# Up projection of a hybrid transformer block: four of seven partial products with joined matmuls

## The chip, the cores and the metric
The kernel runs on one core of one Trainium2 chip. The metric is device time in microseconds (us) of one execution. TensorE (PE) does the matmuls and loads its weights in a separate step (PEld), VectorE (DVE) and ScalarE (ACT) do elementwise work, GpSimd (POOL) and SyncE (SP) issue most of the DMAs. Each engine works through its own list of instructions in order and waits on semaphores for the others.

## The reference
One layer over 512 latent tokens and 256 context tokens of width 2048: modulated RMSNorm, an input projection that feeds an attention branch and a short convolution, an output projection with gated residual, then the gated MLP that this change is about, then a final norm.

```
def conv_ffn(h, w_up, cw, cb, w_down):
    u = dwconv3(h @ w_up, cw, cb)          # h: 512 x 2048, w_up: 2048 x 11008
    a, g = jnp.split(u, 2, axis=-1)
    return (a * jax.nn.silu(g)) @ w_down   # 5504 x 2048
```

Everything is float32. A product is formed from float32r halves: each operand is split into a high part and a low remainder, and the product is hi·hi + hi·lo + lo·hi.

## The kernel before, in words
**The up projection.** Its 11008 columns are 86 tiles of 128, taken in pairs f (one tile of the gate g, one of a). The pairs 0 to 2 are done in rows, k by k, with all 512 tokens per matmul (`row`, tiles `uf`). The pairs 3 to 42, 40 blocks in all, are done by a Strassen scheme of seven products over two halves of the tokens, two halves of the input width and the two column tiles. A block's products are p1 ("11"), p2 ("21"), p6 ("2"), q5 ("1"), p7 ("3"), and, one block later, q4 ("4") and q3 ("22") in `finish`. TensorE's order is p1, p2 of block f, q4, q3 of block f-1, p6, q5, p7 of block f.

Each product (`product`) splits 128x1024 weights into a high part on ACT (L998) and a low part on DVE (L999), and runs eight steps of `mm3` (L185 to L189): three matmuls of 256 columns, that is hi·x_hi, hi·x_lo, lo·x_hi, all into columns 0 to 255 of one PSUM bank. `u19p6l` is the low part of product p6 of block 19. Three buffers of high and of low weights are in turn. The x operands are `hf` (the normed input) and `T` (sums of its halves, made in `t_sums`), each with a tile for the high and one for the low part over 512 tokens.

**What DVE and ACT do with a product.** ACT copies p1, p6 and p7 aside (L1174); DVE makes `cg` from p2 (L1212) and q3 (L1182), and `ca` from q5 (L1224); ACT makes the rest of `ca` from q4 (L1180). `acts` runs the convolution (L1005 to L1007), silu and the gating product (L1015) on `cg` and `ca`. DVE also forms the weight sums of the next products (L1213, L1214).

**What is sent out.** Two finished blocks make a pair, whose seven sums (`pair_sums`, `put`, L1040 to L1044) go to DRAM (`t_d`) as operands of the down projection: ACT casts the high part (L1042), DVE forms the low part (L1043), POOL issues the write. They stand in a queue `bg`, of which `pump(1)` after every product takes one step. The tiles `tp` come from the pool t2, in which two buffers are left for them once `hf` and `T` are all made; a cast into one waits for the write from two puts before.

**The order.** Within what the code asks for, a scheduler sets each engine's list when the program is built. `issue_after` makes one instruction stand behind another in it.

**After the up projection** the down projection does seven tiles plainly (tiles `d`, 512 columns), then 24 steps of the same scheme (tiles `v`), and the final norm.

Of the kernel before, what the change touches and what calls it, by code (L numbers as in the profile page):

```python
# [10 lines left out]
F32 = mybir.dt.float32  # L11
F32R = mybir.dt.float32r
AF = mybir.ActivationFunctionType
ALU = mybir.AluOpType
# [3 lines left out]
P = 128  # L18
D = 2048
T = 512  # L20
# [11 lines left out]
G = 6  # L32
# [40 lines left out]
def block_kernel(ctx, tc, xt, ctxt, ctxn, c, c_ctx, w_ada, small, w_in, w_inc, w_q, w_kv, w_out,  # L73
# [23 lines left out]
    def t2(shape, dt, name):  # L97
        return act.tile(shape, dt, tag="t2", bufs=NT2, name=name)
# [37 lines left out]
        return ap.to_broadcast([P, n])  # L136

    spare = {}
    nth = {"raw": 0, "w": 0}

    ordered = [True]

# [36 lines left out]
    def part(w, i, n=1):  # L179
        return tuple(z[:, i * P:(i + n) * P] for z in w)  # L180
# [4 lines left out]
    def mm3(ps, w, x, first, last, on_top=False):  # L185
        with tc.issue_after(behind.pop()) if behind else ExitStack():
            PE.matmul(ps, w[0], x[0], start=first, stop=False, skip_group_check=on_top)  # L187
        PE.matmul(ps, w[0], x[1], start=False, stop=False, skip_group_check=on_top)  # L188
        PE.matmul(ps, w[1], x[0], start=False, stop=last, skip_group_check=on_top)  # L189


    bg, post, late_bg = deque(), [], []

    def pump(n=1):
        while n and bg:
            if next(bg[0], bg) is bg:
                bg.popleft()
            else:
                n -= 1
# [430 lines left out]
    with ExitStack() as pb:  # L630
# [238 lines left out]
        def bank_of(i, nm):  # L869
            return p8.tile([P, 512], F32, tag=f"s{i}", bufs=1, name=nm)  # L870
# [41 lines left out]
    def whole(raw, xs, nm, ps=None, cols=slice(0, T), ld=None, often=False):  # L912
# [10 lines left out]
            pump(1)  # L923
        return ps

    hf = {}


    hf_last = [None, None]

    def hf_tile(j, cols=slice(0, T)):
        if j not in hf:
# [7 lines left out]
        hi, lo = (z[:, cols] for z in hf[j])  # L940
        A.copy(out=hi, in_=xr)
        ins = V.tensor_tensor(out=lo, in0=xr, in1=hi.bitcast(F32), op=ALU.subtract)
        hf_last[:] = hf_last[1], ins.ins

    def hf_early():
# [89 lines left out]
    def pair_sums(p, e, o):  # L1035


        t = tmp([P, T], F32, f"ts{p}") if p == PAIRS - 1 else cp.tile([P, T], F32, tag="ts", bufs=1, name=f"ts{p}")

        def put(n, src):  # L1040
            z = t2([P, T], F32R, f"tp{p}{n}")
            A.copy(out=z[:, :256], in_=src)  # L1042
            V.tensor_tensor(out=z[:, 256:], in0=src, in1=z[:, :256].bitcast(F32), op=ALU.subtract)  # L1043
            G_.dma_start(t_d[p, OPS.index(n)], z.bitcast(F32))  # L1044

        put("11", e[:, H0])
# [28 lines left out]
    def t_sums(j):  # L1075

        e, o = xres[2 * j], xres[2 * j + 1]
        i, c = j // 2, HS[j % 2]
        if j % 2 == 0:
            for n in (1, 2, 4):  # L1080
                TT[n, i] = tuple(t2([P, T], F32R, f"T{n}{i}{z}") for z in "hl")

        def put(dst, src):
            hi, lo = dst
            A.copy(out=hi, in_=src)
            V.tensor_tensor(out=lo, in0=src, in1=hi.bitcast(F32), op=ALU.subtract)

        V.tensor_tensor(out=e[:, H0], in0=e[:, H0], in1=e[:, H1], op=ALU.subtract)
        V.tensor_tensor(out=e[:, H1], in0=o[:, H1], in1=e[:, H1], op=ALU.subtract)
        put(half_of(hf[2 * j], 1), e[:, H1])  # L1090
        V.scalar_tensor_tensor(out=o[:, H1], in0=e[:, H0], scalar=-1.0, in1=o[:, H1], op0=ALU.mult, op1=ALU.subtract)
        V.scalar_tensor_tensor(out=o[:, H0], in0=o[:, H1], scalar=-1.0, in1=o[:, H0], op0=ALU.mult, op1=ALU.subtract)
        for n, src in ((1, e[:, H0]), (2, o[:, H1]), (4, o[:, H0])):
            put(tuple(z[:, c] for z in TT[n, i]), src)

    def operand(n, j):
        if n in ("11", "3"):
            return half_of(hf[2 * j], n == "3")
        if n in ("21", "22"):
            return half_of(hf[2 * j + 1], n == "22")  # L1100
        return half_of(TT[int(n), j // 2], j % 2)

    def first_weights(k, held=False):

# [8 lines left out]
    def up_load(f):  # L1113
# [7 lines left out]
                G_.dma_start(r[-1], src[more], accum_op=ALU.add)  # L1121
        return r

    pss = [bank_of(i, f"uf{g}") for g, i in enumerate((2, 3, 4, 5, 1, 0))]
    held = [first_weights(k, k > 2) for k in range(EARLY)]
    for k in range(3, EARLY):
        hf_tile(k, H0)
    for k in range(EARLY):
        row(pss, held[k], hf[k], k, H0)
        pump(1)  # L1130
    drain()
    for k in range(EARLY):
        hf_tile(k, H1)
        row(pss, held[k], hf[k], k, H1)
        pump(1)
        if k in (3, 5):
            t_sums(k // 2 - 1)
# [9 lines left out]
    for k in range(EARLY, NK):  # L1147
        w = nxt
        if k + 1 < NK:
            if k == NK - 4:  # L1150
                raws = up_load(G // 2)
            if k == NK - 2:
                t_sums(sums.popleft())
            nxt = prepare(k + 1)
        row(pss, w, hf[k], k)
        if k % 2:
            sums.append(k // 2)
            t_sums(sums.popleft())
# [3 lines left out]
    bank8 = in_turn(BANKS)  # L1162
    one_bank[0] = bank8

    def product(ps, a, n, nm, first):

        w = split4(a, 1024, nm)
        for j in range(8):
            mm3(ps[:, :256], part(w, j), operand(n, j), first and j == 0, j == 7, on_top=not first)
        pump(1)  # L1170

    def aside(ps, nm):
        r = cp.tile([P, 256], F32, tag="uu", bufs=4, name=nm)
        A.copy(out=r, in_=ps[:, :256])  # L1174
        return r

    def finish(st):
        f, a22, s4, u2, u3, pa, pc, cg, ca = st
        product(pa, a22, "4", f"u{f}q4", False)
        A.activation(ca[:, H0], pa[:, :256], AF.Identity, scale=-1.0)  # L1180
        product(pc, s4, "22", f"u{f}q3", False)
        V.tensor_tensor(out=cg[:, H1], in0=pc[:, :256], in1=u2, op=ALU.add)  # L1182
        acts(f, cg, ca)


# [13 lines left out]
    for f in range(G // 2, NF):  # L1199
        a11, a12, s1, s3, a22 = raws  # L1200
        if f + 1 < NF:
            raws = up_load(f + 1)
        else:
            for _ in range(AHEAD):
                plain_fetch()
        pa, pb, pc = (bank8(f"u{f}{z}") for z in "abc")
        cg = cp.tile([P, T], F32, tag="cg", bufs=2, name=f"cg{f}")
        ca = cp.tile([P, T], F32, tag="ca", bufs=2, name=f"ca{f}")
        product(pa, a11, "11", f"u{f}p1", True)
        u1 = aside(pa, f"u{f}1")  # L1210
        product(pb, a12, "21", f"u{f}p2", True)
        V.tensor_tensor(out=cg[:, H0], in0=pb[:, :256], in1=u1, op=ALU.add)  # L1212
        V.tensor_tensor(out=a11, in0=a11, in1=s1, op=ALU.add)  # L1213
        V.tensor_tensor(out=a12, in0=a12, in1=a11, op=ALU.add)  # L1214
        if pend is not None:
            finish(pend)
        if first_acts and f == G // 2:
            acts(*first_acts.pop(0))
        product(pa, a11, "2", f"u{f}p6", False)
        u2 = aside(pa, f"u{f}2")  # L1220
        product(pc, s1, "1", f"u{f}q5", True)
        product(pa, s3, "3", f"u{f}p7", False)
        u3 = aside(pa, f"u{f}3")
        V.scalar_tensor_tensor(out=ca[:, H1], in0=pc[:, :256], scalar=-1.0, in1=u3, op0=ALU.mult, op1=ALU.subtract)  # L1224
        if first_acts:
            acts(*first_acts.pop(0))
        pend = f, a22, a12, u2, u3, pa, pc, cg, ca
# [366 lines left out]
```

## Time and profile before
| | us |
|---|---|
| median of 3 runs | 2151.49 |
| lowest, highest | 2147.65, 2155.0 |
| the profiled execution, its own time | 2158.83 |
| span of its instructions | 2157.0 |
| TensorE busy in the span | 2104.9 |
| VectorE busy | 1769.0 |
| ScalarE busy | 1047.1 |

The granted TensorE clock is 0.994 of full speed over the span. A row of the timeline has an instruction's start and its length; matmuls overlap, so that what one takes of TensorE's time is the distance from its start to the next one's. VectorE's and ScalarE's records overlap a little too.

### The profile page before, as it was taken

Reading aid. Unit: us, or ns where it says so; the run is one execution under the profiler, and the core shown is the slowest. Engines: PE = TensorE matmul, PEld = TensorE weight load, DVE = VectorE, ACT = ScalarE, POOL = GpSimd, SP = SyncE. Lnnn points to the kernel's source line nnn. Section 1 sums busy time; section 2 is a strip of 40 time slices with the busy share of each in tenths; the row PEclk is TensorE's granted clock in tenths of the full one; section 3 lists DMA queues with packets and bytes.
Section 4 is the critical chain, followed back from the end, with each engine's and each line's share of the span. In section 5 each row is a group of like instructions: output and inputs, shape, how many; then the busy total and the mean of one; then the engine's idle time right before and its main releaser. Section 6 shows DMA issues by size and latency. Waiting matters only on the chain.

```text
span 2157.0 us, 37744 instructions
## 1 busy us (share of the span) xinstructions
PE 2104.9 (98%) x14458; PEld 1946.7 (90%) x14458; DVE 1769.0 (82%) x2859; ACT 1047.1 (49%) x1710; POOL 188.1 (9%) x270
## 2 busy tenths in 40 slices
PE   7899999999999999999999999999999999999997
PEld 4688788888888888999999999999999889999997
DVE  7998987778886889788888788788888658888877
ACT  5533333555552237555555555555555333333445
POOL 0000000000000000111211111111111000000000
PEclk9999999999999999999999999999999999999998
DMA  9979785334559986577887877877887999877683
GB/s 335 345 275 337 270 279 176 128 126 162 177 199 348 344 278 192 159 217 201 241 232 215 240 229 220 237 231 219 241 229 218 341 335 290 254 220 236 196 247 111
DMA packets 162121, 513.89 MB, mean 238 GB/s; under 512 B 18962, under 2 KB 23314, under 8 KB 156306
## 3 DMA queue, kind: packets, MB, share of 16 engines
q1 hardware_dynamic: 133364, 418.14, 56.5%
q0 software_dynamic: 27488, 92.29, 18.3%
q8 instruction: 113, 1.85, 0.3%
q10 hardware_dynamic: 1088, 1.05, 0.1%
q14 instruction: 68, 0.56, 0.1%
HBM read 464.22 MB, written 46.14 MB: 237 GB/s over the span
## 4 chain that ended last, share of the span: by engine, by line
PE 86%; DVE 6%; DMA 5%; issue 1%; ACT 1%; SPq 0%; DVEq 0%; POOLq 0%; ACTq 0%
PE pp L187 4%; PE pp L189 4%; PE pp L188 4%; PE o L189 1%; PE o L187 1%; PE o L188 1%; DMA ada<-in_w_ada 1%; PE d L187 1%; PE d L189 1%; PE d L188 1%; PE uf L187 1%; PE uf L188 1%; PE of L187 1%; PE of L188 1%; PE of L189 1%
## 5 line engine op out<-in xcount | busy, mean ns | idle before, releaser
L1044 POOL DMA_DIRECT2D t_d<-tp x126 | 71.9, 574 | 468.3 <-DVE tp L1043 465.4
L255 DVE SCALAR_TENSOR_TENSOR ada<-ada,sv 128x1024 f32<-128x1024 f32 x68 | 82.1, 1219 | 12.1 <-DMA ada<-in_w_ada 12.0
L166 ACT CAST w_0h<-rw 128x512 fp32r<-128x512 f32 (+1 forms) x63 | 38.3, 618 | 108.3 <-PE pp L188 63.1
L1121 POOL DMA_DIRECT2D u_s<-in_w_up x80 | 70.2, 878 | 224.4 <-DMA u_s<-in_w_up 131.5
L233 DVE SCALAR_TENSOR_TENSOR ada<-ada,sv 128x1024 f32<-128x1024 f32 x64 | 77.5, 1217 | 4.4 <-DMA ada<-in_w_ada 3.9
L522 DVE SCALAR_TENSOR_TENSOR ada<-ada,svc 128x1024 f32<-128x1024 f32 x64 | 76.0, 1220 | 2.3 <-DMA ada<-in_w_ada 2.3
L785 POOL TENSOR_TENSOR gr<-gr,half 128x8 f32<-128x8 f32 x4 | 10.1, 2524 | 628.7 <-DVE gr L784 536.8
L1042 ACT CAST tp<-a 128x256 fp32r<-128x256 f32 x90 | 34.7, 405 | 60.5 <-DMA t_d<-tp 54.1
L167 DVE TENSOR_TENSOR w_0l<-rw,w_0h 128x512 fp32r<-128x512 f32 (+1 forms) x63 | 42.6, 681 | 22.3 <-ACT w_0h L166 22.3
L255 DVE SCALAR_TENSOR_TENSOR ra<-ra,sv 128x1024 f32<-128x1024 f32 x44 | 52.5, 1217 | 1.1 <-DMA ra<-in_w_ada 1.1
L1213 DVE TENSOR_TENSOR u<-u,u_s 128x1024 f32<-128x1024 f32 x40 | 48.8, 1219 | 0.7 <-DMA u_s<-in_w_up 0.7
L1214 DVE TENSOR_TENSOR u<-u,u 128x1024 f32<-128x1024 f32 x40 | 48.7, 1218 | 0.0
L1043 DVE TENSOR_TENSOR tp<-a,tp 128x256 fp32r<-128x256 f32 x90 | 36.2, 418 | 12.3 <-ACT tp L1042 12.3
L756 ACT CAST pth<-t 128x384 fp32r<-128x384 f32 x64 | 28.6, 485 | 26.4 <-PE t L753 26.4
L1042 ACT CAST tp<-ts 128x256 fp32r<-128x256 f32 x36 | 14.6, 407 | 43.5 <-DMA t_d<-tp 41.1
L533 DVE TENSOR_TENSOR acc<-acc,pp 128x512 f32<-128x512 f32 x50 | 34.0, 680 | 2.1 <-PE pp L189 2.1
L757 DVE TENSOR_TENSOR ptl<-t,pth 128x384 fp32r<-128x384 f32 x64 | 33.2, 549 | 2.7 <-ACT pth L756 2.7
L737 DVE TENSOR_REDUCE mn<-s 128x1 f32<-128x768 f32 x32 | 30.4, 952 | 4.8 <-PE s L726 4.6
L1043 DVE TENSOR_TENSOR tp<-ts,tp 128x256 fp32r<-128x256 f32 x36 | 15.2, 421 | 23.3 <-ACT tp L1042 23.3
L1005 ACT ACTIVATE g<-cg,sm 128x512 f32<-128x512 f32 x40 | 32.5, 813 | 0.5 <-DVE cg L1182 0.5
L1005 ACT ACTIVATE a<-ca,sm 128x512 f32<-128x512 f32 x40 | 32.1, 803 | 0.0
L1013 ACT ACTIVATE g<-g 128x512 f32<-128x512 f32 x43 | 27.2, 632 | 6.4 <-DVE g L1007 6.4
(15967 smaller groups left out, 9398.2 us busy)
## 6 DMA issues: line engine op xcount, KB each, us to landing
ada<-in_w_ada SPq DMA_DIRECT2D x196, 512.0 KB, 6.0
u<-in_w_up SPq DMA_DIRECT2D x120, 512.0 KB, 8.2
w<-t_d SPq DMA_DIRECT2D x161, 256.0 KB, 5.2
u_s<-in_w_up SPq DMA_DIRECT2D x80, 512.0 KB, 4.3
u_s<-in_w_up POOLq DMA_DIRECT2D x80, 512.0 KB, 8.9
t_d<-tp POOLq DMA_DIRECT2D x126, 256.0 KB, 4.9
v<-in_w_dnw SPq DMA_DIRECT2D x72, 384.0 KB, 5.4
ra<-in_w_ada SPq DMA_DIRECT2D x22, 1024.0 KB, 4.9
```

Of the source, the lines that this page charges most:

```text
L187: PE.matmul(ps, w[0], x[0], start=first, stop=False, skip_group_check=on_top)
L188: PE.matmul(ps, w[0], x[1], start=False, stop=False, skip_group_check=on_top)
L189: PE.matmul(ps, w[1], x[0], start=False, stop=last, skip_group_check=on_top)
L233: V.scalar_tensor_tensor(out=r, in0=r, scalar=1.0, in1=vec[:, i * 1024:(i + 1) * 1024], op0=ALU.mult, op1=ALU.mult, accum_out=col[:, i:i + 1])
L255: keep(V.scalar_tensor_tensor(out=r, in0=r, scalar=1.0, in1=svs[i], op0=ALU.mult, op1=ALU.mult, accum_out=lc[:, t % 4:t % 4 + 1] if i else ...
L522: keep(V.scalar_tensor_tensor(out=raw[q], in0=raw[q], scalar=1.0, in1=svc[:, q * 1024:(q + 1) * 1024], op0=ALU.mult, op1=ALU.mult, accum_o ...
L1005: A.activation(u, src, AF.Identity, bias=s("fb", m), scale=s("fw", 86 + m))
L1042: A.copy(out=z[:, :256], in_=src)
L1043: V.tensor_tensor(out=z[:, 256:], in0=src, in1=z[:, :256].bitcast(F32), op=ALU.subtract)
L1044: G_.dma_start(t_d[p, OPS.index(n)], z.bitcast(F32))
L1121: G_.dma_start(r[-1], src[more], accum_op=ALU.add)
L1213: V.tensor_tensor(out=a11, in0=a11, in1=s1, op=ALU.add)
```

## The change
In the products "21", "1", "4" and "22" the first two matmuls of each step, which have the same weights, become one of 512 columns (`mm2`, L196), for which x_hi and x_lo stand side by side in one tile; the third keeps 256 (L197). The bank then holds hi·x_hi + lo·x_hi in columns 0 to 255 and hi·x_lo in columns 256 to 511, and a new DVE instruction (`beside`, L1207) adds or subtracts the second half after the first has been used. The operands "21" and "22" (odd `hf` tiles) and "1", "2", "4" (`T`) are laid out so; "11" and "3" (even tiles) stay apart. For odd k the row-wise part works by 256 columns.

Beside this, `pump` takes a step after every second product, each third `tp` comes from a buffer of its own (`tq`), its cast stands behind the last high cast of weights, and `ca` has one buffer in place of two.

```
+    def mm2(ps, w, x, first, last, on_top=False):
+        n = x.shape[1] // 2
+        with tc.issue_after(behind.pop()) if behind else ExitStack():
+            PE.matmul(ps[:, :2 * n], w[0], x, start=first, stop=False, skip_group_check=on_top)
+        PE.matmul(ps[:, :n], w[1], x[:, :n], start=False, stop=last, skip_group_check=on_top)
...
+    def side_by_side(z, src):
+        n = T // 2
+        A.copy(out=z[:, :n], in_=src)
+        return V.tensor_tensor(out=z[:, n:], in0=src, in1=z[:, :n].bitcast(F32), op=ALU.subtract)
...
         def put(n, src):
-            z = t2([P, T], F32R, f"tp{p}{n}")
-            A.copy(out=z[:, :256], in_=src)
+            nth["tp"] += 1
+            if nth["tp"] % 3 or p == PAIRS - 1:
+                z = t2([P, T], F32R, f"tp{p}{n}")
+            else:
+                z = cp.tile([P, T], F32, tag="tq", bufs=1, name=f"tp{p}{n}")
+            with tc.issue_after(last_hi[0]):
+                A.copy(out=z[:, :256], in_=src)
...
+    def up_row(w, k, hs=(0, 1)):
+        if k % 2 == 0:
+            row(pss, w, hf[k], k, slice(hs[0] * 256, hs[-1] * 256 + 256))
+            return
+        for g in range(G):
+            for h in hs:
+                mm3(pss[g][:, HS[h]], w[g], two(hf[k, h]), False, k == NK - 1 and h == 1)
...
+    APART = ("21", "1", "4", "22")
+    def beside(dst, ps, minus=False):
+        V.tensor_tensor(out=dst, in0=dst, in1=ps[:, 256:], op=ALU.subtract if minus else ALU.add)
...
         w = split4(a, 1024, nm)
         for j in range(8):
-            mm3(ps[:, :256], part(w, j), operand(n, j), first and j == 0, j == 7, on_top=not first)
-        pump(1)
+            x = operand(n, j)
+            if n in APART:
+                mm2(ps, part(w, j), x, first and j == 0, j == 7, on_top=not first)
+            else:
+                mm3(ps[:, :256], part(w, j), x if isinstance(x, tuple) else two(x), first and j == 0, j == 7, on_top=not first)
+        nth["up"] += 1
+        pump(nth["up"] % 2)
...
         A.activation(ca[:, H0], pa[:, :256], AF.Identity, scale=-1.0)
+        beside(ca[:, H0], pa, True)
         product(pc, s4, "22", f"u{f}q3", False)
         V.tensor_tensor(out=cg[:, H1], in0=pc[:, :256], in1=u2, op=ALU.add)
+        beside(cg[:, H1], pc)
...
-        ca = cp.tile([P, T], F32, tag="ca", bufs=2, name=f"ca{f}")
...
         V.tensor_tensor(out=cg[:, H0], in0=pb[:, :256], in1=u1, op=ALU.add)
+        beside(cg[:, H0], pb)
...
+        ca = cp.tile([P, T], F32, tag="ca", bufs=1, name=f"ca{f}")
         V.scalar_tensor_tensor(out=ca[:, H1], in0=pc[:, :256], scalar=-1.0, in1=u3, op0=ALU.mult, op1=ALU.subtract)
+        beside(ca[:, H1], pc, True)
```

TensorE's list at the start of product p2 of block 20, before (u20b is its bank, u20p2h and u20p2l its weights):

```order
L187 MATMUL u20b<-hf1h,u20p2h 128x256
L188 MATMUL u20b<-hf1l,u20p2h 128x256
L189 MATMUL u20b<-hf1h,u20p2l 128x256
L187 MATMUL u20b<-hf3h,u20p2h 128x256
L188 MATMUL u20b<-hf3l,u20p2h 128x256
L189 MATMUL u20b<-hf3h,u20p2l 128x256
```

And the same place now:

```order
L196 MATMUL u20b<-hf_7575,u20p2h 128x512
L197 MATMUL u20b<-hf_7575,u20p2l 128x256
L196 MATMUL u20b<-hf_7676,u20p2h 128x512
L197 MATMUL u20b<-hf_7676,u20p2l 128x256
L196 MATMUL u20b<-hf_7691,u20p2h 128x512
L197 MATMUL u20b<-hf_7691,u20p2l 128x256
```

Three instructions have become two with the same 768 columns; over the whole program TensorE's list goes from 14099 to 12909 rows.

VectorE's list from the low part of u20p6 to the convolution of block 19, before (cg_12354 and ca_12355 belong to block 19, u_12518 is its product p6 set aside):

```order
L999 TENSOR_TENSOR u20p6l<-u_11_12339,u20p6h 128x1024
L1043 TENSOR_TENSOR tp_12669<-ts_12513,tp_12669 128x256
L999 TENSOR_TENSOR u20q5l<-u_s_12343,u20q5h 128x1024
L1043 TENSOR_TENSOR tp_12704<-a_12480,tp_12704 128x256
L1182 TENSOR_TENSOR cg_12354<-u19c,u_12518 128x256
L1061 SCALAR_TENSOR_TENSOR a_12480<-ts_12513,a_12480 128x256
L999 TENSOR_TENSOR u20p7l<-u_s_12346,u20p7h 128x1024
L1006 SCALAR_TENSOR_TENSOR g_12743<-cg_12354,sm,g_12743 128x511
```

And now (cg_12011 and ca_12219 belong to block 19, cg_12237 to block 20; L1207 is the new add):

```order
L1207 TENSOR_TENSOR ca_12219<-ca_12219,u19c 128x256
L1075 TENSOR_TENSOR tp_12289<-a_11903,tp_12289 128x256
L1263 TENSOR_TENSOR cg_12237<-u20b,u_12266 128x256
L1024 TENSOR_TENSOR u20p6l<-u_11_11996,u20p6h 128x1024
L1207 TENSOR_TENSOR cg_12237<-cg_12237,u20b 128x256
L1024 TENSOR_TENSOR u20q5l<-u_s_12000,u20q5h 128x1024
L1075 TENSOR_TENSOR tp_12406<-ts_12157,tp_12406 128x256
L1207 TENSOR_TENSOR ca_12219<-ca_12219,u19a 128x256
L1233 TENSOR_TENSOR cg_12011<-u19c,u_12162 128x256
L1207 TENSOR_TENSOR cg_12011<-cg_12011,u19c 128x256
L1024 TENSOR_TENSOR u20p7l<-u_s_12003,u20p7h 128x1024
L1031 SCALAR_TENSOR_TENSOR g_12345<-cg_12011,sm,g_12345 128x511
```

The four new adds stand between the low part of q3 and that of p7; one step of the sums sent out stands here in place of two.

## Rows read from the trace of the kernel before

**Rows 1.** The page, part 1: busy us, share of span, instructions of each engine.
```profile
PE 2104.9 (98%) x14458; PEld 1946.7 (90%) x14458; DVE 1769.0 (82%) x2859; ACT 1047.1 (49%) x1710; POOL 188.1 (9%) x270
```

**Rows 2.** Busy us (instructions) in stretches: PE, PEld, DVE, ACT, POOL, clock, DMA.
```profile
900.00:1650.00 750.00, 750.00 (x6252) 750.00 (x6252) 621.63 (x823) 429.95 (x644) 133.96 (x199) 1.00 0.80 226
...
1686.00:1750.00 64.00, 63.72 (x298) 52.77 (x299) 32.36 (x57) 21.44 (x32) 4.10 (x7) 1.00 0.98 358
...
2070.00:2157.00 87.00, 70.69 (x562) 68.48 (x561) 64.86 (x102) 44.64 (x81) 2.55 (x3) 0.94 0.51 154
```

**Rows 3.** PE's waits from 815 us to the end: us in total, times, longest.
```profile
PE v23a L187 <- ACT v23p6h L998: 1.7, 1, 1.7
PE d L187 <- ACT dw00h L998: 1.0, 1, 1.0
PE v19a L189 <- DVE v19q4l L999: 0.9, 1, 0.9
...
PE uf L187 <- ACT ufw0h L998: 0.9, 1, 0.9
```

**Rows 4.** Timeline of PE in product q4 of block 13: start us, length us.
```profile
1106.22 0.28 PE L187 MATMUL u13a<-T40h,u13q4h 128*128 128x256 f32 x1
...
1107.90 0.28 PE L189 MATMUL u13a<-T42h,u13q4l 128*128 128x256 f32 x1
```

**Rows 5.** Timeline of PE in the plain part of the down projection.
```profile
1721.83 0.39 PE L188 MATMUL d<-yl5l,dw05h 128*128 128x512 f32 x1
...
1723.92 0.40 PE L189 MATMUL d<-yl5h,dw05l 128*128 128x512 f32 x1
```

**Rows 6.** Timeline of PE in the attention, 512 columns followed by 256.
```profile
530.97 0.40 PE L723 MATMUL s<-kl20l,q20h 128*128 128x512 f32 x1
531.20 0.28 PE L187 MATMUL po<-pth,v10h 128*128 128x256 f32 x1
531.32 0.27 PE L188 MATMUL po<-ptl,v10h 128*128 128x256 f32 x1
```

**Rows 7.** Timeline of DVE over one block, with [idle before <-releaser].
```profile
1208.08 0.42 DVE L1212 TENSOR_TENSOR cg<-u19b,u 128x256 f32<-128x256 f32 x1
1208.41 1.22 DVE L999 TENSOR_TENSOR u19p6l<-u,u19p6h 128x1024 fp32r<-128x1024 f32 x1
1211.06 1.23 DVE L999 TENSOR_TENSOR u19q5l<-u_s,u19q5h 128x1024 fp32r<-128x1024 f32 x1 [1.44 <-ACT u19q5h L998]
1212.98 0.42 DVE L1182 TENSOR_TENSOR cg<-u18c,u 128x256 f32<-128x256 f32 x1 [0.69 <-PE u18c L189]
1213.94 1.23 DVE L999 TENSOR_TENSOR u19p7l<-u_s,u19p7h 128x1024 fp32r<-128x1024 f32 x1 [0.54 <-ACT u19p7h L998]
...
1228.40 1.23 DVE L999 TENSOR_TENSOR u20p6l<-u,u20p6h 128x1024 fp32r<-128x1024 f32 x1 [0.52 <-ACT u20p6h L998]
```

**Rows 8.** Timeline of PE: first uses of u19p2l and u19p6l.
```profile
1204.38 0.28 PE L189 MATMUL u19b<-hf1h,u19p2l 128*128 128x256 f32 x1
...
1213.02 0.28 PE L189 MATMUL u19a<-T20h,u19p6l 128*128 128x256 f32 x1
```

**Rows 9.** Timeline of ACT and DVE ahead of u19p2l.
```profile
1199.68 0.41 ACT L1042 CAST tp<-a 128x256 fp32r<-128x256 f32 x1 [2.78 <-DMA t_d<-tp]
...
1202.20 1.22 DVE L999 TENSOR_TENSOR u19p2l<-u,u19p2h 128x1024 fp32r<-128x1024 f32 x1
```

**Rows 10.** ACT's waits from 884 to 1686 us, the longest.
```profile
ACT tp L1042 <- DMA t_d<-tp: 95.2, 62, 2.9
```

**Rows 11.** Busy us in a stretch of blocks 4 and 5, columns as in rows 2.
```profile
912.00:930.00 18.00, 18.00 (x152) 18.00 (x152) 18.00 (x23) 11.64 (x18) 3.12 (x5) 1.00 0.71 191
```

More of the change, by code (lines that the diff above doesn't have):

```diff
@@ L138, in block_kernel @@
     spare = {}
-    nth = {"raw": 0, "w": 0}
+    nth = {"raw": 0, "w": 0, "up": 0, "tp": 0}
     ordered = [True]
@@ L926, in block_kernel, with two @@
     hf = {}
+    def side_by_side(z, src):
+        n = T // 2
+        A.copy(out=z[:, :n], in_=src)
+        return V.tensor_tensor(out=z[:, n:], in0=src, in1=z[:, :n].bitcast(F32), op=ALU.subtract)
+    def two(z):
+        return z[:, :T // 2], z[:, T // 2:]
     hf_last = [None, None]
     def hf_tile(j, cols=slice(0, T)):
-        if j not in hf:
+        if j % 2 == 0 and j not in hf:
             hf[j] = tuple(t2([P, T], F32R, f"hf{j}{z}") for z in "hl")
@@ L939, in hf_tile @@
         A.activation(xr, xr, AF.Identity, bias=mod[:, 48 + j:49 + j], scale=sc)
-        hi, lo = (z[:, cols] for z in hf[j])
-        A.copy(out=hi, in_=xr)
-        ins = V.tensor_tensor(out=lo, in0=xr, in1=hi.bitcast(F32), op=ALU.subtract)
+        if j % 2 == 0:
+            hi, lo = (z[:, cols] for z in hf[j])
+            A.copy(out=hi, in_=xr)
+            ins = V.tensor_tensor(out=lo, in0=xr, in1=hi.bitcast(F32), op=ALU.subtract)
+        else:
+            for h in range(2):
+                if cols in (HS[h], slice(0, T)):
+                    hf[j, h] = t2([P, T], F32R, f"hf{j}{h}")
+                    ins = side_by_side(hf[j, h], xres[j][:, HS[h]])
         hf_last[:] = hf_last[1], ins.ins
@@ L1040, in put @@
         def put(n, src):
-            z = t2([P, T], F32R, f"tp{p}{n}")
-            A.copy(out=z[:, :256], in_=src)
+            nth["tp"] += 1
+            if nth["tp"] % 3 or p == PAIRS - 1:
+                z = t2([P, T], F32R, f"tp{p}{n}")
+            else:
+                z = cp.tile([P, T], F32R, tag="tq", bufs=1, name=f"tp{p}{n}")
+            with tc.issue_after(last_hi[0]):
+                A.copy(out=z[:, :256], in_=src)
             V.tensor_tensor(out=z[:, 256:], in0=src, in1=z[:, :256].bitcast(F32), op=ALU.subtract)
@@ L1077, in t_sums @@
         e, o = xres[2 * j], xres[2 * j + 1]
[L1078 to L1081, printed above, removed]
+        for n in (1, 2, 4):
+            TT[n, j] = t2([P, T], F32R, f"T{n}{j}")
         def put(dst, src):
@@ L1093, in t_sums @@
         for n, src in ((1, e[:, H0]), (2, o[:, H1]), (4, o[:, H0])):
-            put(tuple(z[:, c] for z in TT[n, i]), src)
+            put(two(TT[n, j]), src)
     def operand(n, j):
@@ L1099, in operand @@
         if n in ("21", "22"):
-            return half_of(hf[2 * j + 1], n == "22")
-        return half_of(TT[int(n), j // 2], j % 2)
+            return hf[2 * j + 1, int(n == "22")]
+        return TT[int(n), j]
     def first_weights(k, held=False):
@@ L1128, in block_kernel @@
     for k in range(EARLY):
-        row(pss, held[k], hf[k], k, H0)
+        up_row(held[k], k, (0,))
         pump(1)
@@ L1133, in block_kernel @@
         hf_tile(k, H1)
-        row(pss, held[k], hf[k], k, H1)
+        up_row(held[k], k, (1,))
         pump(1)
@@ L1154, in block_kernel @@
             nxt = prepare(k + 1)
-        row(pss, w, hf[k], k)
+        up_row(w, k)
         if k % 2:
@@ L1168, in product @@
         for j in range(8):
-            mm3(ps[:, :256], part(w, j), operand(n, j), first and j == 0, j == 7, on_top=not first)
-        pump(1)
+            x = operand(n, j)
+            if n in APART:
+                mm2(ps, part(w, j), x, first and j == 0, j == 7, on_top=not first)
+            else:
+                mm3(ps[:, :256], part(w, j), x if isinstance(x, tuple) else two(x), first and j == 0, j == 7, on_top=not first)
+        nth["up"] += 1
+        pump(nth["up"] % 2)
     def aside(ps, nm):
```

## The prediction
> **What bounds the kernel now.** I read the busy times first: TensorE works 98% of the span, VectorE 82%, ScalarE 49% [rows 1]. Then the stretches: between 900 and 1650 us, the steady part of the up projection, TensorE is busy 750.00 of 750 us at a clock of 1.00, VectorE 621.63 [rows 2]. A busy TensorE may still be one that crawls, so third came its waits: over everything after 815 us the longest are for the first weights of the up and the down projection and for steps of the tail (v19 and later); no tile of the seven-product blocks is among them [rows 3]. Last the timeline, for the pace: from 1106.22 to 1107.90 there are 14 steps, 0.120 us each [rows 4]. A block has 7 x 24 = 168 matmuls, so 168 x 0.120 = 20.16 us, and the 40 blocks take 806 us. TensorE alone sets that time, matmul behind matmul, and what the change is worth is read from the price of a matmul and from whether the other engines still keep ahead.
>
> **The joined matmuls.** A step of a product was three matmuls of 256 columns, 3 x 0.120 = 0.360 us. Now it is one of 512 and one of 256, the same 768 columns. What 512 columns cost is seen where they run back to back without waits: nine steps from 1721.83 to 1723.92 us, 2.09 / 9 = 0.232 us [rows 5]. A 512 followed by a 256, as it will be here, is seen in the attention: 0.23 us to the next start, and the 256 behind it 0.12 [rows 6]. So a step comes to between 0.350 and 0.352 us and saves 8 to 10 ns; I take 9. Four products of eight steps in 40 blocks are 1280 steps: 10 to 12.8 us less, 11.5 taken. A matmul thus costs its columns and some ns for being one, and 1280 of these small sums go.
>
> The Trainium skill (TensorE: Matmul & The Clock Gate, Back-to-back issue gap) gives for a lone stream N/2.4 + 2.5 ns. By that a joined step saves one 2.5 ns, 3.2 us in all, an estimate from that page. The trace disagrees on both levels: the page would have 109 and 216 ns where the rows have 120 and 232.
>
> **The split rows.** For the odd tiles 7 to 15 the row-wise part now works by 256 columns: 5 tiles x 6 banks x 3 = 90 matmuls become 180. At 8 to 10 ns each that is 0.7 to 0.9 us back; 0.8 taken. ScalarE and VectorE make the halves of those five tiles apart, ten instructions more, in a stretch where TensorE runs without a wait [rows 3]; nothing.
>
> **The new adds.** VectorE gets four of 128x256 a block, one operand in PSUM, the form of L1212. That one reads 0.42 us, and the next starts 0.33 us after it [rows 7]; so 4 x 0.33 = 1.3 us a block. In the steady part VectorE works 621.63 / 37.2 = 16.7 us of each 20.16 (750 / 20.16 = 37.2 blocks) and is idle 3.45. It would work 18.0 of about 19.9, with 1.9 idle. Load alone doesn't decide it, since its list is in order; the place does. The rows show four idle times in one block: 1.44 us before u19q5l, 0.69 before cg, 0.54 before u19p7l, 0.52 before u20p6l [rows 7]. All are waits for work that TensorE or ScalarE hadn't done: VectorE is ahead there. The new list puts the add to block 20's cg just before u20q5l, in the place of the 1.44; those to ca and cg of block 19 around cg, in the place of 0.69 and 0.54; the fourth ahead of u20p6l, in the place of 0.52. Each of the four idle times is longer than 0.33.
>
> What that cover is worth if it fails: behind a late add stands the low part of the next weights, and TensorE waits for it at the third matmul of mm3 or the second of mm2. u19p6l is ready at 1208.41 + 1.22 = 1209.63 and first used at 1213.02, 3.4 us later [rows 7, 8]. All four adds together are shorter than that. The thinnest place I found is u19p2l, ready at 1203.42 and used at 1204.38, 0.96 us [rows 8, 9]; none of the new adds stands between the low part of p1 and that of p2, and what made it late was ScalarE's wait of 2.78 us for a write of sums sent out [rows 9]. Bounds for the adds: nothing, or 1.3 us in each of 40 blocks, 54 us; I take nothing, since the idle rows are the nearest.
>
> One place has no idle rows. In blocks 4 and 5 VectorE is busy 18.00 of 18.00 us [rows 11], because the convolutions of the first three pairs fall there. Four adds and the faster TensorE (0.3 us a block) can cost 0 to 1.6 us, once; I take 0.4.
>
> **The sums sent out.** Per two blocks there are 14 products and seven sums; a step after every second product is seven steps, just enough, so the queue doesn't grow, and the work is the same. What moves is spacing: two casts no longer fall together, and every third has a buffer of its own, so the 62 waits of ScalarE, 95.2 us in all and up to 2.9 each [rows 10], get shorter. TensorE waits behind none of them today, so this earns nothing; it thickens the thin place above. Moving the cast behind the weights' high cast does likewise. Queued behind it on ScalarE are only the copies and the next high cast, and POOL's writes take the sums in the same number. Bounds 0 to -1, taken 0.
>
> **One ca buffer.** The subtraction into the next ca (L1224) must now wait until the convolution of the last one has read it. Both stand on VectorE, the reader first, and ScalarE's read of ca is earlier still; the low part of q3 is what queues behind. Nothing.
>
> **Transfers and the end.** The same bytes are sent in 10 us less. The stretch 1686 to 1750 us runs the DMA engines at 0.98 with TensorE busy 63.72 of 64 [rows 2]; its loads hang on buffers that TensorE's progress frees, so they come earlier with it. SP's list is a little different there, the second plain weights ahead of some operands. In the last 87 us TensorE is idle 16.3 us [rows 2] and two matmuls change place. Each may give or take 1 us; I take 0.
>
> **Sum.** -11.5 + 0.8 + 0.4 = -10.3 us. The profiled execution takes 2158.83 us with a span of 2157.0 and would come to 2148.5, the span to 2146.7. The median of the three runs is 2151.49, 7 below the profiled one; the difference carries over, as the steady part is the same: 2141 us.
>
> **Rivals.**
> *Gain eaten.* The joined matmul costs as much as two of 256 in this place, 0.240, or the blocks lose a quarter us each to VectorE. For it: TensorE had 98% and no rival's stall was ever seen, so small stalls of 0.2 us a block have no row to rule them out; VectorE goes to 91%. Against it: 0.23 in the mixed row and 0.232 in the other. Time: 2151.5 + 0.8 = 2152 at no gain, 2147 at half.
> The gap that the Trainium skill (TensorE: Matmul & The Clock Gate, Back-to-back issue gap) states would bring the time here too: 2151.5 - 3.2 + 0.2 = 2148, an estimate from that page (the split rows at its 2.5 ns); it lies among this rival's times and gets no chance beside its.
>
> *VectorE becomes the bound.* The place is its list between the low part of q3 and that of p7. If the idle 3.45 us a block are not slack but waits that each add pushes along (a later cg makes ScalarE's g later, that makes VectorE's convolution wait), a block takes VectorE's 18.0 plus what idle is left. From 20.16 - 18.0 = 2.1 us of kept idle on it is slower than before. With 2.5 kept a block takes 20.5, 40 x 0.4 = 16 us more: 2167. With all of it 21.5, 2204. For it: VectorE's waits come back in every block. Against it: high parts are made by ScalarE from TensorE's progress, and whoever comes later to such a wait waits less.
>
> *More than the sum.* The low price per step (0.350), a shorter tail and thinner waits: -12.8 + 0.9 - 1.5 = -13.4, 2138.
>
> **How the numbers follow.** Forecast, 2138 to 2145: 0.60. Gain eaten, 2145 to 2153: 0.22. VectorE the bound: 0.10, most of it above 2153. More than the sum: 0.08. What can be told from no change is 0.3%, 6.5 us: 2145 to 2158. Forecast and the better case are faster (0.68), and of the eaten ones those near 2145 may count so, 0.03 in all; 0.71 faster. The rest of the eaten, 0.19, is the same, and of VectorE's case 0.01; 0.20. Slower 0.09. The range: below, 2138 less the 3.8 by which the lowest run lies under the median, 2134; above, no gain at all and a little more, 2153. Outside stand VectorE's case and a tail, under 0.2.
>
> **What the changed profile would show.** In the steady stretch TensorE still busy throughout, starts 0.23 and 0.12 apart in the joined products, a block 19.9 us; VectorE at about 0.91 with its idle before q5l and p7l smaller by the adds; ScalarE's waits for writes well below 95 us; the down projection's first matmul some 10 us earlier. Wrong would be the forecast if waits of TensorE for low parts of u tiles appear in its list of waits, if a 512 takes 0.240, or if the loads at 1686 us leave it idle.

## The result and the profile after

The changed kernel takes 2159.29 us (median of 9 runs, 2153.73 to 2165.17), the one before 2151.49 beside it (2144.96 to 2155.52). The ratio is 1.0037, 95% interval 1.0021 to 1.0054: slower by some 8 us where 10 us less were forecast. One correction to the diff shown above: the tile `tq` has the type F32R in the code, not F32.

First the page, part 1, of the changed kernel, in the columns of [rows 1]:

```profile
PE 2095.5 (97%) x13268; PEld 1883.6 (87%) x13268; DVE 1825.5 (85%) x3024; ACT 1046.5 (49%) x1715; POOL 187.9 (9%) x270
```

Then its steady stretch, in the columns of [rows 2]:

```profile
900.00:1650.00 750.00, 736.22 (x4980) 682.57 (x4979) 661.77 (x954) 420.14 (x630) 131.05 (x194) 0.99 0.78 222
```

TensorE was busy 750.00 of 750 us before; now it is idle 13.8, and the clock is 0.99. A fall from 1.00 to 0.99 is small in print, but an average over 750 us hides short falls to half. The joined steps themselves run as forecast, here in TensorE's timeline (start, length; the pace is from start to start):

```profile
1028.96 0.39 PE L196 MATMUL u10c<-T,u10q5h 128*128 128x512 f32 x1
1029.18 0.28 PE L197 MATMUL u10c<-T,u10q5l 128*128 128x256 f32 x1
1029.31 0.40 PE L196 MATMUL u10c<-T,u10q5h 128*128 128x512 f32 x1
```

One step is 1029.31 - 1028.96 = 0.35 us. What is new stands in the list of TensorE's waits from 815 us on (total, times, longest), which answers to [rows 3]:

```profile
PE u36a L187 <- ACT u L1224: 2.5, 1, 2.5
PE u18a L187 <- ACT u L1224: 2.3, 1, 2.3
PE u24a L187 <- ACT u L1224: 2.3, 1, 2.3
PE u30a L187 <- ACT u L1224: 2.1, 1, 2.1
PE u10a L187 <- ACT u L1224: 2.0, 1, 2.0
PE u12a L187 <- ACT u L1224: 2.0, 1, 2.0
PE v23a L187 <- ACT v23p6h L1023: 1.7, 1, 1.7
...
PE u29b L197 <- DVE u29p2l L1024: 0.3, 1, 0.3
PE u26a L197 <- DVE u26q4l L1024: 0.2, 1, 0.2
```

Six blocks have a stall of 2.0 to 2.5 us, 13.2 us together. TensorE waits there to begin p7 (L187) in the bank that holds p6, until ScalarE has copied p6 aside (L1224). Two short waits for low parts of weights come to 0.5 us more. Before, no tile of a seven-product block stood in this list. What made the copy late is read in block 10, from the chain of waits, start and length:

```profile
1017.32 3.89 DMA u_s<-in_w_up
1021.25 0.50 issue
1021.77 0.56 POOL u_s L1151
1022.34 10.37 DMA t_d<-tp
1033.04 0.38 ACT u L1224
1033.46 0.58 PE u10a L187
```

and from ScalarE's timeline, with [idle before <-releaser]:

```profile
1028.39 1.06 ACT L1023 CAST u11p1h<-u 128x1024 fp32r<-128x1024 f32 x1
1032.73 0.41 ACT L1074 CAST tp<-a 128x256 fp32r<-128x256 f32 x1 [3.29 <-DMA t_d<-tp]
1033.04 0.37 ACT L1224 COPY u<-u10a 128x256 f32<-128x256 f32 x1
```

and POOL's:

```profile
1021.77 0.89 POOL L1151 DMA_DIRECT2D u_s<-in_w_up  x1 [1.17 <-DMA u_s<-in_w_up]
1022.34 0.88 POOL L1076 DMA_DIRECT2D t_d<-tp  x1
```

Read from the end: p7 waits for the copy; the copy stands in ScalarE's list behind a cast of a sum, ready to run long before; the cast waits 3.29 us until the write that last used its tile has landed; that write was issued on POOL's queue directly behind a load that accumulates onto weights (u_s), and took 10.37 us. The other five read alike. In each of the six the write was issued 0.57 us behind such a load and took 9.7 to 10.4 us, and TensorE's stall is 1.29 us shorter than the cast's wait (2.00 of 3.29 us here, 2.51 of 3.80 in block 36): that is the slack of what stands behind the cast.

The other part of the price is the clock. TensorE's granted clock in the 3.4 us behind two of the six stalls (columns as in [rows 2], the clock after the bracket of POOL):

```profile
1033.40:1036.80 3.40, 3.34 (x15) 3.34 (x16) 3.22 (x5) 1.47 (x3) 0.55 (x1) 0.50 0.81 283
1200.60:1204.00 3.40, 3.40 (x18) 3.40 (x18) 3.22 (x5) 0.38 (x2) 0.00 (x0) 0.50 0.66 224
```

All six read 0.50 or 0.51, that is 1.2 GHz in place of 2.4: the work of 1.7 us takes 3.4. So the six stalls cost 13.2 + 6 x 1.7 = 23.4 us. By the first matmul of block 3 and the first of the plain part, the seven-product blocks take 801.8 us before and 812.0 after, where the forecast's terms make 801.8 - 11.5 + 0.4 = 790.7; the 21.3 us between are about these 23.4.

Last, ScalarE's longest waits from 884 to 1690 us, against [rows 10]:

```profile
ACT tp L1074 <- DMA t_d<-tp: 53.2, 16, 4.5
```

and the DMA part of the page (KB each, median us from issue to landing), before:

```profile
t_d<-tp POOLq DMA_DIRECT2D x126, 256.0 KB, 4.9
```

and after:

```profile
t_d<-tp POOLq DMA_DIRECT2D x126, 256.0 KB, 8.6
```

The median landing rose since more writes stand right behind an accumulating load on POOL's queue. Those issued within 2 us of one take 10.0 us (56 of 126) and the others 5.1; in the kernel before it was 10.2 (18 of 126) and 4.7. The sum of the waits fell from 95.2 to 53.2 us and their number from 62 to 16, as forecast; the longest rose from 2.9 to 4.5. The total is the wrong column here, and the longest is so too: what reaches TensorE is each wait less the slack of what stands behind it. The longest, 4.5 us, stood in block 28 ahead of an activation of g (L1038) and cost TensorE, by way of VectorE, the 0.3 us for u29p2l in the list above; the six that cost over 2 us each are waits of 3.3 to 3.8 us.

The two profiled executions differ by 0.2 us (2157.0 and 2157.2), the medians by 7.8: the one before was profiled in a run 7 us over its median. Places are read from the profiles, the sizes of the verdicts from the medians.

### The profile page after: what moved, and what is told of

Its sections match the earlier page's. It is cut to its first block, busy times and chain, and to the rows that moved or that the text cites. A ratio compares the mean times of both kernels' runs of the same rounds, so it can differ in the third digit from the quotient of the medians.

```text
span 2157.2 us, 35425 instructions
## 1 busy us (share of the span) xinstructions
PE 2095.5 (97%) x13268; PEld 1883.6 (87%) x13268; DVE 1825.5 (85%) x3024; ACT 1046.5 (49%) x1715; POOL 187.9 (9%) x270
## 4 chain that ended last, share of the span: by engine, by line
PE 78%; DMA 11%; DVE 7%; issue 2%; ACT 2%; POOL 0%; DVEq 0%; SPq 0%; POOLq 0%; ACTq 0%
DMA t_d<-tp 4%; PE pp L187 4%; PE pp L189 4%; PE pp L188 3%; DMA u_s<-in_w_up 3%; DMA ada<-in_w_ada 2%; PE o L189 1%; PE o L187 1%; PE o L188 1%; PE d L187 1%; PE d L189 1%; PE d L188 1%; PE uf L187 1%; PE uf L188 1%; PE uf L189 1%
## 5 line engine op out<-in xcount | busy, mean ns | idle before, releaser
L1076 POOL DMA_DIRECT2D t_d<-tp x126 | 81.1, 657 | 442.5 <-DVE tp L1075 431.5
L1074 ACT CAST tp<-a 128x256 fp32r<-128x256 f32 x90 | 35.9, 406 | 67.6 <-DMA t_d<-tp 53.2
L1038 ACT ACTIVATE g<-g 128x512 f32<-128x512 f32 x43 | 27.2, 632 | 15.2 <-DVE g L1032 14.8
L748 ACT ACTIVATE p<-s,mn 128x768 f32<-128x768 f32 x32 | 29.3, 915 | 1.6 <-DVE mn L745 1.3
L1032 DVE SCALAR_TENSOR_TENSOR a<-ca,sm,a 128x511 f32<-128x511 f32 x40 | 29.9, 747 | 0.0
```

## The experiments

The theory: joining is worth what was forecast; the loss comes from a cast of a sum that stands in ScalarE's list ahead of the copy of p6 and waits for a late write. Its rivals: the four adds overload VectorE; the joined matmul is dearer than the rows said.

**The copy ahead of the cast.** The changed kernel; the queue's step is taken at the start of the next product, after the last result was copied aside, and the cast is put behind that copy.

```
+        nth["up"] += 1
+        pump(nth["up"] % 2)
         w = split4(a, 1024, nm)
...
-        nth["up"] += 1
-        pump(nth["up"] % 2)
...
-        A.copy(out=r, in_=ps[:, :256])
+        last_hi[:] = [A.copy(out=r, in_=ps[:, :256]).ins]
```

> The changed kernel, with the step of the sums sent out taken after a product's result has been set aside, not before it, and its cast put behind that copy on ScalarE; so no cast stands ahead of the copy of p6 that p7 waits for. Theory (order): the six stalls of TensorE before p7, 2.0 to 2.5 us each and each followed by 3.4 us at half clock, come from a cast that waits for a late write and stands ahead of that copy. Then no stall is left, and the time is about 2141 us, ratio to before 0.995. Rival (VectorE's load): the adds make TensorE late, and the ratio stays at 1.003. Rival (the writes' rhythm itself, whatever the order): 1.003 too, with writes landing in 8 to 9 us as in the changed kernel.

2138.07 us (2135.58 to 2140.17), ratio 0.9928 [0.9911, 0.9945]: faster than both kernels. ScalarE's timeline at the same place:

```profile
1028.63 1.06 ACT L1023 CAST u11p1h<-u 128x1024 fp32r<-128x1024 f32 x1
1029.60 0.36 ACT L1223 COPY u<-u10a 128x256 f32<-128x256 f32 x1
1029.85 0.41 ACT L1074 CAST tp<-ts 128x256 fp32r<-128x256 f32 x1
```

TensorE's waits:

```profile
PE v23a L187 <- ACT v23p6h L1023: 1.7, 1, 1.7
PE u42a L196 <- ACT u L1223: 1.3, 1, 1.3
```

and the steady stretch:

```profile
900.00:1650.00 750.00, 750.00 (x5163) 697.37 (x5162) 686.02 (x989) 439.53 (x654) 135.45 (x200) 1.00 0.83 230
```

The copy runs at 1029.60 and not 1033.04, TensorE is busy throughout at full clock, and VectorE does all four adds a block at 686.02 / 750 = 91%. The rival of VectorE's load falls with this. The casts hardly wait for writes any more either (twice, 0.6 us in all). Fewer of POOL's writes stand right behind an accumulating load, 32 of 126 in place of 56. In its timeline the one at 1006.19 still does, those at 1020.66 and 1032.71 don't:

```profile
1005.65 0.85 POOL L1151 DMA_DIRECT2D u_s<-in_w_up  x1 [2.63 <-DMA u_s<-in_w_up]
1006.19 0.88 POOL L1076 DMA_DIRECT2D t_d<-tp  x1
...
1020.66 0.54 POOL L1076 DMA_DIRECT2D t_d<-tp  x1 [1.23 <-DVE tp L1075]
1023.18 0.89 POOL L1151 DMA_DIRECT2D u_s<-in_w_up  x1 [1.98 <-DMA u_s<-in_w_up]
1025.99 0.87 POOL L1151 DMA_DIRECT2D u_s<-in_w_up  x1 [1.93 <-DMA u_s<-in_w_up]
1032.71 0.58 POOL L1076 DMA_DIRECT2D t_d<-tp  x1 [5.85 <-DVE tp L1075]
```

So this run cures the order and the casts' waits together and does not part them.

**Joined matmuls alone.** The matmuls and adds of the change, the sums sent out as before.

```
-            nth["tp"] += 1
-            if nth["tp"] % 3 or p == PAIRS - 1:
-                z = t2([P, T], F32R, f"tp{p}{n}")
-            else:
-                z = cp.tile([P, T], F32R, tag="tq", bufs=1, name=f"tp{p}{n}")
-            with tc.issue_after(last_hi[0]):
-                A.copy(out=z[:, :256], in_=src)
+            z = t2([P, T], F32R, f"tp{p}{n}")
+            A.copy(out=z[:, :256], in_=src)
...
-        nth["up"] += 1
-        pump(nth["up"] % 2)
+        pump(1)
```

> Joined matmuls and the four adds, but the sums sent out as in the kernel before: a step after every product, tiles from the common pool only, no place behind the high cast. Order theory and writes' rhythm: 0.995, about 2141 us, no stall, writes landing in about 5 us. VectorE's load: 1.00 or more, as the adds are all there.

2210.61 us, ratio 1.0269 [1.0244, 1.0295]: a miss, and a large one. Its waits of TensorE:

```profile
PE u13a L187 <- ACT u13p1h L1023: 4.2, 1, 4.2
PE u25a L187 <- ACT u25p1h L1023: 4.1, 1, 4.1
PE u41a L187 <- ACT u41p1h L1023: 4.0, 1, 4.0
```

Here the waiting cast stands ahead of the high part of p1, which TensorE needs at once: ScalarE's list has 15 such places, where the kernel before has none. ScalarE waits 124.0 us for writes, 53 times, up to 5.6. Thus the joined matmuls alone move the scheduler's list as well; the expectation had taken the order for that of before.

**The same, with the cast put behind the last high cast.** One edit from the run above:

```
+            with tc.issue_after(last_hi[0]):
                 A.copy(out=z[:, :256], in_=src)
```

> e2 (joined matmuls, sums sent out after every product through the two tiles of the common pool) with one edit: the cast of a sum stands behind the last high cast of weights. In e2's list 15 casts of sums stand ahead of the high cast of p1 and 49 ahead of that of p6; here none and 2, most are ahead of q3 and q5, as in the kernel before. Theory (what stands behind the waiting cast on ScalarE decides): TensorE's waits for p1 go, and 1.027 becomes 0.994 to 1.000, though the casts wait as long in all. Rival (the waits' sum, or VectorE's load): it stays above 1.015.

2147.56 us, ratio 0.9975 [0.9959, 0.9992]. TensorE's largest wait in the blocks:

```profile
PE u41b L196 <- ACT u41p2h L1023: 1.5, 1, 1.5
```

and ScalarE's for the writes:

```profile
ACT tp L1069 <- DMA t_d<-tp: 95.9, 57, 4.2
```

ScalarE still waits 57 times and up to 4.2 us, and the writes still land late (7.8 us), yet 63 us are gone. What stands behind the waiting cast decides, not how long ScalarE waits in all. In this list no cast stands ahead of the copy of p6; so the cast's place behind the last high cast does not by itself put it there. Which of the other parts of the new sending does was not undone one by one.

**The new sending alone.** The kernel before with the steps after every second product, the own tile for every third, the cast behind the last high cast and one `ca` buffer; no joined matmuls.

```
-        pump(1)
+        nth["up"] += 1
+        pump(nth["up"] % 2)
...
-            z = t2([P, T], F32R, f"tp{p}{n}")
-            A.copy(out=z[:, :256], in_=src)
+            nth["tp"] += 1
+            if nth["tp"] % 3 or p == PAIRS - 1:
+                z = t2([P, T], F32R, f"tp{p}{n}")
+            else:
+                z = cp.tile([P, T], F32R, tag="tq", bufs=1, name=f"tp{p}{n}")
+            with tc.issue_after(last_hi[0]):
+                A.copy(out=z[:, :256], in_=src)
...
-        ca = cp.tile([P, T], F32, tag="ca", bufs=2, name=f"ca{f}")
...
+        ca = cp.tile([P, T], F32, tag="ca", bufs=1, name=f"ca{f}")
```

> The kernel before with the new sending only (a step after every second product, each third tile its own, the cast behind the high cast, one ca buffer), and no joined matmul. In this program no cast stands ahead of a copy set aside. Order theory: 1.000, no stall in the up projection, though writes land late. Writes' rhythm: 1.005 to 1.01, since nothing is gained to pay for it. VectorE's load: 1.000.

2168.98 us, ratio 1.0066 [1.0040, 1.0091]. The expectation had the list wrong: ScalarE's list of this kernel does have casts ahead of the copy of p6, in 17 blocks. Its stalls stand at 11 of them, for instance

```profile
PE u38a L187 <- ACT u L1181: 2.6, 1, 2.6
PE u26a L187 <- ACT u L1181: 2.0, 1, 2.0
PE u16a L187 <- ACT u L1181: 1.8, 1, 1.8
```

All 11 casts that wait there wait for a write that POOL issued 0.57 us behind an accumulating load and that took 9.7 to 11.2 us. So the loss is there without one joined matmul or new add: the step at fault is the sending.

**The writes of the sums issued by SP.** One edit, to the changed kernel and to the kernel with the new sending alone:

```
-            G_.dma_start(t_d[p, OPS.index(n)], z.bitcast(F32))
+            SP.dma_start(t_d[p, OPS.index(n)], z.bitcast(F32))
```

> The changed kernel with the sums' writes issued by SyncE and not by GpSimd, so that they don't stand behind the accumulating weight loads in one queue. If the writes land late because of that queue, they land in 3 to 5 us here, the casts wait less, the stalls go, and the time is 0.995 to 1.00, the upper end if SyncE's waiting for the sums holds up the weights. If the landing has nothing to do with the queue, 8 to 9 us stay. VectorE's load: 1.003.

> The kernel before with the new sending (a step after every second product, every third from a tile of its own, the cast behind the last high cast), no joined matmuls, and the writes of the sums issued by SP in place of POOL. ScalarE's list has the same 17 casts of sums ahead of the copy of p6 as with POOL's writes. If the queue is what makes the writes late (they stand behind accumulating weight loads on POOL's): no or one stall before p7 in place of eleven, landing 3 to 6 us in place of 7.8, ScalarE's waits for writes under 10 us, and a ratio of 0.998 to 1.002. If the order alone were the cause: eleven stalls and 1.006 as with POOL's writes.

With the joined matmuls 2142.28 us, 0.9949 [0.9931, 0.9968], where POOL's writes gave 1.0037; without them 2156.71, 1.0022 [1.0007, 1.0038], where they gave 1.0066. Both lists have a cast ahead of the copy of p6 in 17 blocks, as the new sending alone had it with POOL's writes (the changed kernel: in 7). What is left of the first one's stalls (TensorE) and of its waits for writes (ScalarE):

```profile
PE u28a L187 <- ACT u L1224: 1.3, 1, 1.3
...
ACT tp L1074 <- DMA t_d<-tp: 2.1, 1, 2.1
```

The second has none, its writes land in 6.0 us, and its blocks take 801.8 us, as before. So the order alone is harmless while the cast finds its write landed: it needs both, the place in ScalarE's list and a late write for the cast that stands there. Late writes as such are not POOL's alone. On SP's queue those within 2 us behind a load of weights (u) took 10.2 us in the second kernel, 37 of the 93 whose landing the trace has, but no cast waited for one of them. In the first the writes land in 6.1 us, over the 3 to 5 expected. The two cures together, the copy first and the writes by SP, add nothing to the first cure:

> The step of the sums after the copy (as in e1) and the writes issued by SyncE (as in e4). If what is left in e1 are waits for writes, this is a little faster than e1, 0.992; if SyncE's waiting holds up the weights, as VectorE's waits of 29 us for accumulated weights in e4 speak for, it is as e4, 0.995.

2139.96 us, ratio 0.9939 [0.9913, 0.9965].

**More tiles.** Three own tiles in place of one, so that a cast waits for an older write; the room for them came from the raw weights' buffers, 8 in place of 9.

```
-        return rw.tile([P, 1024], F32, tag="raw", bufs=9, name=nm)
+        return rw.tile([P, 1024], F32, tag="raw", bufs=8, name=nm)
...
-            if nth["tp"] % 3 or p == PAIRS - 1:
+            if nth["tp"] % 5 < 2 or p >= PAIRS - 2:
...
-                z = cp.tile([P, T], F32R, tag="tq", bufs=1, name=f"tp{p}{n}")
+                z = cp.tile([P, T], F32R, tag="tq", bufs=3, name=f"tp{p}{n}")
```

> The changed kernel with three tiles of their own for the sums in place of one, five in turn with the two of the common pool; to make room, the weights' raw tiles are eight in place of nine. A cast then waits for the write from five puts before. In its list 18 casts stand ahead of the copy of p6, more than in the changed kernel. Theory (a cast that waits for a late write holds up what ScalarE has behind it): with no such wait the order doesn't matter, TensorE has no stall before p7, though writes still land in 8 to 9 us, and the ratio is 0.993 to 0.996. Rival (the order alone, or the late landing alone): stalls in the 18 places, 1.003 or more. One raw tile less may cost a little.

2242.56 us, ratio 1.0408 [1.0386, 1.0430]. No wait for the copy of p6 is left, but others took their place, so the run alone told nothing. Its control has the eight raw buffers and nothing else new:

> The changed kernel with eight buffers for raw weights in place of nine, nothing else: a control for the run with three own tiles, which had to give up one raw buffer to find the room and took 1.041. If the missing raw buffer was its cost: about 1.04, VectorE waiting some 100 us or more for accumulated weights (u_s, L1265) and TensorE for low parts behind them, besides the stalls before p7. If the three own tiles were the cost: about 1.004 as the changed kernel, with its six stalls of 2.0 to 2.5 us before p7.

2246.39 us, ratio 1.0441 [1.0418, 1.0465]. VectorE's waits from 884 to 1690 us in it, and the first of TensorE's in the blocks:

```profile
DVE u L1265 <- DMA u_s<-in_w_up: 125.1, 34, 5.4
...
PE u6b L197 <- DVE u6p2l L1024: 3.3, 1, 3.3
```

One raw buffer less costs 4%: VectorE then waits for accumulated weights and TensorE for low parts. That is the whole loss of the run with three tiles. This control has no wait for the copy of p6 either, where the expectation kept the six stalls; so their absence from the run before says nothing of the tiles. Whether more tiles alone would cure the stalls stays open.

**What joining is worth.** The version with the copy first, without the joined matmuls:

> The kernel before with the new sending, the step taken behind the copy set aside and the cast placed behind that copy, as in the fastest version so far (0.9928), but no joined matmuls. The difference between the two is what joining is worth where no cast holds up a copy. Forecast's term: 10.7 us, so 0.998 here. If the placing of the casts earned by itself, beyond the loss it takes away: below 0.995. If joining is worth more than its term, through a faster pace of all matmuls: 1.000 or above, with a pace of 0.120 us for 256 columns here.

2157.23 us, ratio 1.0020 [1.0007, 1.0034]. This is the third case of the expectation, 1.000 or above with a pace of 0.120 us. With the joined matmuls it was 0.9928: joining gives 0.92%, 19.8 us. The pair with SP's writes gives 1.0022 - 0.9949 = 0.73%, 15.7 us. By the intervals each is known to some 5 us. Both are over the forecast's 10.3. Where it lies, by the first matmuls of the parts, in us, for these four kernels, none of which has a stall in the blocks above 1.3 us (blocks and plain tiles are told together, since up to two products of block 42 stand behind the first plain matmul, and not the same number in each kernel):

| | blocks 3 to 42 and seven plain tiles | v0 to v16 | 256 behind 256, mean |
|---|---|---|---|
| copy first, not joined | 886.0 | 238.1 | 0.1200 |
| copy first, joined | 870.6 | 236.3 | 0.1186 |
| writes by SP, not joined | 885.7 | 237.6 | 0.1200 |
| writes by SP, joined | 873.4 | 235.0 | 0.1186 |

Blocks and plain tiles gain 15.4 and 12.3 us, against 11.1 forecast (11.5 less 0.4). In the copy-first pair that is the joined steps (0.351 in place of 0.360 us, 1280 times, 11.6 us) and the pace of the matmuls that were not joined, 0.1186 in place of 0.1200 us: 72 a block in 40 blocks make 2880 x 0.0014 = 4.0 us. The SP pair has 1.3 us less by the stall at u28a; the rest of the difference was not located. What lies outside the blocks can't be put down to joining: v0 to v16 takes 235.1 us in the kernel with the new sending alone, which has no joined matmul, and 238.4 in the one with both cures, which has them.

Both versions without joined matmuls are 0.2% (4 to 5 us) slower than the kernel before, though they have no stall above 1.3 us in the blocks. The profiles do not show where.

**The kernel before once more**, for the spread between two profiles:

> The kernel before once more, unchanged, for a second trace of it: whether its matmuls of 256 columns again start 0.120 us apart, or 0.119 as in the changed kernel and the experiments, also in the down projection where nothing was changed. If 0.120 belongs to that program, it is 0.120 here; if it is a matter of the execution, 0.119 may stand here. No theory on the stalls speaks of it.

One execution of 2156.74 us, its span 2154.9; blocks 801.8 as in the first profile, the pace 0.1200 again. The uf tiles start at 812.9 against 815.2, so a difference of 2 us in one part between two profiles says nothing by itself.

## Why the prediction was wrong

**The step that failed** is "The sums sent out": "TensorE waits behind none of them today, so this earns nothing; it thickens the thin place above. Moving the cast behind the weights' high cast does likewise. ... Bounds 0 to -1, taken 0." It measured +23.4 us in the changed kernel (13.2 of stalls and 10.2 of half clock; the copy-first version, without them, is 1.09% or some 23 us faster). Two things in it were not followed to their end. The step named "the copies" as queued behind the cast and did not ask who waits for a copy: p7 does, since it accumulates in p6's bank. In block 20, whose lists the prediction draws on for VectorE, the copy comes first in ScalarE's list; in seven others the cast stands ahead of it, and in six of these it waited and TensorE stalled. And it counted POOL's writes as "the same number" without asking what they now stand behind on POOL's queue: 56 in place of 18 right behind an accumulating load, where a write lands in some 10 us and not in 5. Both are needed, a cast ahead of the copy and a late write for it, as the pairs with SP's writes show. The prediction's own row for this was at hand: the 2.78 us wait of ScalarE in [rows 9], which it held to be the cause of the thinnest place, is longer than the 2.0 to 2.5 us that reached TensorE now. Below nothing was bounded (-1), above nothing not at all, though the change moves an instruction that waits for a DMA, and a wait of 2.9 us stood in [rows 10].

**Joined matmuls: right.** 0.350 to 0.352 us a step forecast; the means in the changed kernel are 0.231 for a 512 and 0.120 for the 256 behind it, 0.351. That makes 11.6 us against 11.5. The 4.0 us by which the other matmuls ran faster were not in the forecast. That the cured kernels (0.9928 and 0.9949, which is 2136 and 2141 us on 2151.5) meet the forecast of 2141 is so in part luck: they have this gain, and they have the 0.2% of the new sending that was taken at nothing.

**Split rows: right.** From the first uf matmul to the first of block 3 the pair with the copy first has 69.2 us unjoined and 69.9 joined: 0.7 against 0.8.

**The adds: right.** The version with the copy first has every add in it and takes 0.9928; no wait of TensorE for a low part in the blocks stands in its list, and VectorE works 91% there, as forecast. The changed kernel has two such waits, 0.5 us together.

**One `ca` buffer: right as far as seen**; no wait for it stands in the lists. It was not undone by itself.

**Transfers and the end: right within its bounds of 1 us** in the plain tiles (83.9 before, 84.1 after). The rest of the down projection and the tail took 7.0 us less (v0 to the end 386.9 and 379.9), more than the forecast gave them; v0 to v16 has 3.3 of it, with the pace of 0.1187. This can't be put down to the change: the same stretch takes 384.5 us in the second profile of the kernel before and 380.1 with the new sending alone.

**The rivals.** VectorE as the bound had the sign of the result but not its mechanism. Its first price is a little high besides: 20.5 - 20.16 = 0.34 us in 40 blocks is 13.6 us, so 2165 and not 2167. "Gain eaten" was for small stalls without a row; what came was six stalls with a row each. What was said to show the forecast wrong (waits for low parts, a 512 at 0.240, loads at 1686 us) held little of it. Waits for low parts of u tiles did appear, but only the two of 0.3 and 0.2 us, and the larger came from a late cast and not from an add; the copy aside was missing from the list.

## What to carry to other kernels

When a change moves an instruction that waits for a DMA, read the in-order list behind it over all blocks, and follow each thing that stands there to whoever waits for it. Each wait counts against the slack of what stands right behind it; neither the sum of the waits nor the longest tells the price. Then read the DMA's own queue: what a transfer stands behind is part of its time. Put what feeds TensorE (copies that free a bank, high parts of weights) ahead of work that can be late, and test two edits that came together one at a time, since each may move the scheduler's list.

## What was not expected of the hardware

A stall of 2.0 to 2.5 us was followed by 3.4 us at half clock in six of six cases in the changed kernel. In the kernel with the new sending alone, 11 stalls of 0.9 to 2.6 us were followed by it only twice, once here, behind one of 1.8 us:

```profile
1161.30:1164.70 3.40, 3.40 (x19) 3.40 (x18) 2.28 (x4) 0.36 (x1) 0.00 (x0) 0.50 0.43 161
```

One of 2.0 us there was not followed by it, and in the run with joined matmuls alone three of 15 stalls before p1 (2.2 to 2.5 us) were not. What parts them was not settled.

A 256 KB write of a sum that POOL issued within 2 us behind an accumulating load landed in 8.9 to 10.6 us at the median of each run with POOL's writes, the kernel before included (10.2); in the changed kernel such a write landed 0.5 to 2.7 us after the load. All 16 casts that waited in the changed kernel and all 11 in the one with the new sending alone waited for such a write. SP's queue shows the like behind loads of weights (10.2 us). So 7.8 us at the median with POOL and 6.0 with SP, with the same order of the casts (the two kernels without joined matmuls), goes with what a write stands behind; the longest of either queue is near 13.

The pace of matmuls of 256 columns has two values at full clock, 0.1200 and 0.1187 us, and it changes within one execution. In the kernel with the new sending alone it is 0.1200 in the blocks up to the first stall (1037 us), 0.1187 from there to the stall at 1160, 0.1200 up to the stall at 1244, and 0.1187 from then on to the end of the blocks. The kernels without joined matmuls and without a stall up to block 41 keep 0.1200 through the blocks, the kernel before in both profiles; those with joined matmuls have 0.1186 to 0.1191. So it is not fixed by the program alone; its cause is open.
